# Layer-1 mixer: substitution of the 16x16 blocks per head group, spreads placed behind a convolution, second q-v-part last

## The chip, the cores and the metric

The kernel runs on one core of a Trainium2 chip. The metric is the device time of one execution in microseconds (us). Five instruction streams matter: TensorE (PE in the rows; its weight loads are PEld), VectorE (DVE), ScalarE (ACT), GpSimd (POOL) and SyncE (SP, which issues the weight loads). Each engine runs its own stream in order; a stream goes on when the semaphores that it waits for have come.

## The reference, cut to what matters

The reference is a trunk of two layers, each mixer, cross-attention and gated MLP with layer norms, on 256 tokens of width 1024. The change lies in the mixer of layer 1, a gated DeltaNet of 8 heads in chunks of 64 tokens:

```python
qkv = jax.nn.silu(causal_dwconv(jnp.concatenate([q, k, v], axis=-1), conv_w))   # width 4, per channel
m = jnp.where(strict, jnp.einsum('bhntk,bhnsk->bhnts', kb, kh) * decay, 0.0)
tinv = lax.linalg.triangular_solve(eye + m, eye, left_side=True, lower=True, unit_diagonal=True)
u = jnp.einsum('bhnts,bhnsv->bhntv', tinv, vh * beta[..., None])
w = jnp.einsum('bhnts,bhnsk->bhntk', tinv, kb * jnp.exp(gc)[..., None])
# over the chunks: v_new = u - w S;  out = qg S + qk v_new;  S = S * g_last + kg^T v_new
```

`q`, `k`, `v` and `z` come from one product of the tokens with `w_in`. For each head and chunk a unit lower triangular 64x64 matrix is inverted (`tinv`), which needs only `k` and the decays; `q` and `v` come in after it.

## The kernel before, in words

Eight heads are two groups of four (`grp`), 256 tokens are two tiles of 128 (`tt`); a unit of the chain below is one group and one tile, thus four heads by two chunks of 64.

TensorE's program in this mixer is written out by hand. `weave` runs a **chain** (the recurrence of `mixer_c`) and a **fill** (projections that nobody in the chain needs at once). Each yield of the chain says how many fill steps go in before its next part, and the table `NW` (L35) gives the weights; one step of a projection is six matmuls of 256 columns (`ps_t`, L159 to L161) or three of 512 (`ps_n`, L165 to L167). The fill is, in order, the projections q0, v0, q1, v1 (name and group), then z1. What the other engines do is put in their streams by a scheduler, roughly in the order in which the program names it. A projection piece of 24 matmuls costs VectorE and ScalarE this: ScalarE casts a weight block to `wh` (L152), VectorE takes the rest `wl` (L154), and when the piece's PSUM bank is full ScalarE starts the convolution `cv` (L927), VectorE adds three shifted terms (L930, called a convolution's three parts below) and ScalarE applies silu (L935). Such a bank is free again only after the third part, and there are four of them.

The chain, in the order of L1240 to L1262: `gdn_pre_k` of both groups makes the transposed matrix `LT` on VectorE (L1046), stores it to a scratch tensor in DRAM (`scr_in`, L1050, a queue of GpSimd) and transposes it back to `L`. `base_solve` (L1080 to L1099) loads the 128 diagonal 16x16 blocks, one on each partition (`base`, L1085), inverts them by substitution in 28 small instructions on GpSimd (L1087 to L1093), stores them (`scr_out`, L1094) and loads them back as `zc` with four DMAs, one per unit (L1099). `gdn_pre_q` makes what `q` and `v` give. `gdn_inv` first spreads `zc` into the block diagonal of `Z` (L1108, two instructions per unit on VectorE) and then doubles the block size in three levels: `pA` from `Z`, a masked copy `A` on VectorE, `pX`, a copy `X` on ScalarE, `pZ`, and `Z` anew on VectorE; at the end `pw`. `gdn_rec` is the recurrence over the chunks. All of VectorE's work for chain and fill stands in one stream.

The order is: pre_k of group 0, pre_k of group 1, one solve for both groups, wait for v0 in the fill, pre_q of group 0, wait for q1 in the fill, the inversion of group 0, wait for v1, pre_q of group 1, then the inversion of group 1 side by side with the recurrence of group 0, the rest of the fill, and the recurrence of group 1.

Of the kernel before, what the change touches and what calls it, by code (L numbers as in the profile page):

```python
# [10 lines left out]
F32 = mybir.dt.float32  # L11
# [3 lines left out]
ALU = mybir.AluOpType  # L15
AX = mybir.AxisListType

P = 128
D = 1024
KT = D // P  # L20
T = 256
# [8 lines left out]
BASE = 16  # L30
# [1 line left out]
LAG = 4  # L32
NEARLY = 6
AHEAD = 2
NW = [3, 2.6, 1, 1.5, 0.8, 1, 1, 1, 0.5, 8, 4, 1, 6, 2, 0, 5.2, 0.8, 3]  # L35
NEG = -1e30

def _constants():
# [51 lines left out]
def hybrid_trunk(ctx: ExitStack, tc: tile.TileContext, a: dict, const: dict, out: bass.AP, dbg=None):  # L90
    nc = tc.nc
# [7 lines left out]
    lnp = ctx.enter_context(tc.tile_pool(name="lnp", bufs=2))  # L99
# [26 lines left out]
    def C(name):  # L126
        group, c0, n = _COLS[name]
        return csb[group][:, c0:c0 + n]
# [40 lines left out]
    def run(gen):  # L169
        for _ in gen:  # L170
            pass
# [101 lines left out]
    def steps(n, *gens):  # L273

        gens = list(gens)
        while gens:
            due = 0
            for gen in list(gens):
                m = next(gen, gens)
                if m is gens:  # L280
                    gens.remove(gen)
                else:
                    due += n if m is None else m
            yield due
# [113 lines left out]
    def new_h():  # L398
        return [hp.tile([P, D], F32, tag="h", name="h") for _ in range(2)]
# [106 lines left out]
    def mixer_ab(h, hT, ap_, fill, res):  # L506
# [54 lines left out]
        with pool("gla") as sm:  # L561
# [124 lines left out]
            def intra(u):  # L686
# [4 lines left out]
                for l in range(NLEV + 1):  # L691
# [8 lines left out]
                    if l in (2, 4):  # L700
                        yield NW[14]
                pk = mm("pk")[:, :P]
# [36 lines left out]
            def gla():  # L739
# [7 lines left out]
                for i, u in enumerate(units):  # L747
                    yield from intra(u)
                    yield NW[15]
                    if i % 2:  # L750
# [28 lines left out]
            yield 0  # L779
            yield from steps(NW[1], gla())  # L780

# [87 lines left out]
    def mixer_c(h, hT, sm, smq, fill, res):  # L869
# [4 lines left out]
        cw = conv_w[0]  # L874
# [46 lines left out]
            table.append(nc.scalar.activation(egs.rearrange("p a b -> p (a b)"), pg[:, :32], AF.Exp))  # L921

        gate = [x.rearrange("p (t d) -> p t d", t=2) for x in new_h()]

        def conv_silu(dst, m, ps, late):
            y = smq.tile([P, T], F32, tag="cv", name="cv", bufs=4)
            nc.scalar.mul(y, ps, cw[:, 3, m:m + 1])  # L927
            for j in range(3):
                d = 3 - j
                nc.vector.scalar_tensor_tensor(y[:, d:], ps[:, :T - d], cw[:, j, m:m + 1], y[:, d:],  # L930
                                               op0=ALU.mult, op1=ALU.add)

            def finish():
                with tc.issue_after(table[0].ins):
                    table[1:] = [nc.scalar.activation(dst, y, AF.Silu)]  # L935
            late.append(finish) if late is not None else finish()
# [22 lines left out]
            return smq.tile(B4, F32, tag="t2", name=name, bufs=5)  # L959

        scr = ctx.enter_context(tc.tile_pool(name="scr", bufs=1, space=bass.MemoryType.DRAM))
        scr_in = scr.tile([16, P * (P + 1)], F32, name="scr_in")
        scr_out = scr.tile([P, BASE * BASE], F32, name="scr_out")

        os_ = [[{}, {}], [{}, {}]]

# [27 lines left out]
        tts = nc.vector.tensor_tensor  # L994
# [12 lines left out]
        def gdn_pre_k(grp, tt, o):  # L1007

            tsl = slice(tt * P, tt * P + P)
            cs = slice(tt * 8 + grp * 4, tt * 8 + grp * 4 + 4)  # L1010
            k = qkvT["k", grp][:, :, tsl]
            sc = o["sc"] = sm.tile([P, 6, 4], F32, tag="sc", name="sc", bufs=4)

            pg = bank("pg")
            mm4(pg, lambda g: gg[:, tt, grp * 4 + g:grp * 4 + g + 1].broadcast_to([P, P]), lambda g: tri)
            pk = bank("pk")
            tr4(pk, k)
            dT = o["att"] = keep("dT", grp, tt)
            for g in range(4):
                i = tt * 8 + grp * 4 + g  # L1020
                nc.vector.scalar_tensor_tensor(dT[:, g], pg[:, g], ngc[:, i:i + 1], dmask, op0=ALU.add, op1=ALU.min)
            with tc.issue_after(table[1].ins):
                nc.scalar.activation(dT, dT, AF.Exp)
                if tt:
                    qg = o["qg"] = keep("kq", grp, tt)
                    nc.scalar.activation(qg, pg, AF.Exp)
            sum_sq(sc[:, 0], pk)
            if tt:
                kgx = o["kgx"] = sm.tile(B4, F32, tag="kgx", name="kgx")
                tts(kgx, pk, col(egs[:, 0, cs]), op=ALU.mult)  # L1030
            else:
                kg = o["kg"] = keep("kq", grp, tt)
                tts(kg, pk, col(egs[:, 1, cs]), op=ALU.mult)
            yield


            nc.vector.tensor_scalar(sc[:, 0], sc[:, 0], RMS_EPS, None, op0=ALU.add)
            nc.gpsimd.tensor_tensor(sc[:, 2], sc[:, 0], phalf, op=ALU.pow)
            nc.vector.reciprocal(sc[:, 3], sc[:, 0])
            nc.vector.tensor_tensor(sc[:, 3], sc[:, 3], beta[:, tt, grp * 4:grp * 4 + 4], op=ALU.mult)  # L1040
            o["b"], o["eq"] = sc[:, 3], sc[:, 4]
            pK = bank("pK")
            mm4(pK, lambda g: k[:, g], lambda g: k[:, g])
            LT = t2("LT")
            for g in range(4):
                nc.vector.scalar_tensor_tensor(LT[:, g], pK[:, g], sc[:, 3, g:g + 1], dT[:, g],  # L1046
                                               op0=ALU.mult, op1=ALU.mult)
            yield

            nc.gpsimd.dma_start(scr_in[grp * 8 + tt * 4:grp * 8 + tt * 4 + 4, :P * P].rearrange("g (s t) -> s g t", t=P), LT)  # L1050
            pL = bank("pL")
            tr4(pL, LT)
            L = o["L"] = smq.tile(B4, F32, tag="L", name="L", bufs=4)
            nc.scalar.copy(L, pL)
            yield
# [21 lines left out]
            tts(dT, pQ, dT, op=ALU.mult)  # L1077
            yield

        def base_solve():  # L1080

            src = scr_in.rearrange("a b -> (a b)").rearrange("(p x) -> p x", x=BASE * (P + 1))
            src = src[:, :BASE * P].rearrange("p (i t) -> p i t", t=P)[:, :, :BASE]
            m, z = lnp.tile([P, 512], F32, tag="tok", name="base").rearrange("p (a i j) -> a p i j", a=2, j=BASE)
            nc.gpsimd.dma_start(m, src)  # L1085
            eng = nc.gpsimd
            eng.tensor_scalar(z, m, -1.0, None, op0=ALU.mult)  # L1087
            for i in range(1, BASE - 1):
                sh = [P, i, BASE - 1 - i]
                t = sm.tile([P, 64], F32, tag="bt", name="bt")[:, :sh[1] * sh[2]].rearrange("p (i j) -> p i j", i=i)  # L1090
                eng.tensor_tensor(t, z[:, :i, i:i + 1].broadcast_to(sh), m[:, i:i + 1, i + 1:].broadcast_to(sh), op=ALU.mult)
                eng.tensor_tensor(z[:, :i, i + 1:], z[:, :i, i + 1:], t, op=ALU.subtract)
            eng.memset(z.rearrange("p i j -> p (i j)")[:, ::BASE + 1], 1.0)  # L1093
            nc.gpsimd.dma_start(scr_out, z.rearrange("p i j -> p (i j)"))  # L1094
            back = scr_out.rearrange("(u g b) (i j) -> u (b i) g j", u=4, g=4, j=BASE)
            zc = sm.tile([P, 4, 4, BASE], F32, name="zc", bufs=1)
            for u in range(4):
                os_[u // 2][u % 2]["zc"] = zc[:, u]
                nc.gpsimd.dma_start(zc[:, u], back[u])  # L1099

        def gdn_inv(o):

            zc, L = o["zc"], o["L"]

            Z = o["Z"] = t2("Z")
            for u in range(2):
                sh = [P, 4, BASE, 4]
                tts(Z[:, :, 64 * u:64 * u + 64].rearrange("p g (r b) -> p g r b", b=4),  # L1108
                    zc.unsqueeze(3).broadcast_to(sh),
                    C("blocks")[:, 4 * u:4 * u + 4].unsqueeze(1).unsqueeze(1).broadcast_to(sh), op=ALU.mult)  # L1110
            for lev in range(4, NLEV + 1):

                last = lev == NLEV
# [30 lines left out]
                else:  # L1144
                    tts(Zv[:, :, :, 1], packed(Z[:, :, 64:]), packed(pZ), op=ALU.subtract)
                    Z = o["Z"] = Z2
# [82 lines left out]
        def until(nm, grp):  # L1229

            while (nm, grp) not in made:
                yield 1
            yield LAG

        def units(n, gen, grp, *args):
            return steps(n, *(gen(grp, tt, os_[grp][tt]) for tt in range(2)))

        def inv(grp):
            return [gdn_inv(os_[grp][tt]) for tt in range(2)]

        yield 0
        fill.gens += [fills(), proj_z(1)]
        yield from units(NW[3], gdn_pre_k, 0)
        yield from units(NW[5], gdn_pre_k, 1)
        base_solve()
        yield from until("v", 0)
        yield from units(NW[7], gdn_pre_q, 0)
        yield from until("q", 1)
        yield from steps(NW[4], *inv(0))
        yield from until("v", 1)  # L1250
        yield from units(NW[8], gdn_pre_q, 1)
        outs = []
        yield from steps(NW[16], *inv(1), gdn_rec(0, os_[0], outs))
        fill.rest()
        new = new_t("oT")
        oT.hi, oT.lo = new.hi, new.lo
# [2 lines left out]
        outs = []  # L1259
# [243 lines left out]
```

## Time and profile before

| | us |
|---|---|
| three runs | 935.9, 934.82, 934.26; median 934.82 |
| the profiled execution: its own time | 933.78 |
| its span in the trace | 931.9 |
| TensorE busy in it | 898.1 (96 %) |
| VectorE busy | 680.2 |
| ScalarE busy | 517.7 |
| GpSimd busy | 54.6 |

A time in a row counts from the span's start. A row of instructions in order of time gives its start, its length, engine, line, operation, tiles and the number merged into it; in brackets stands the idle time ahead of it and who ended that. "PEclk" is TensorE's granted clock as a share of full speed: 1.00 is 2.4 GHz, 0.50 is 1.2 GHz. A row on a stretch gives its bounds, its length, the busy time of PE, PEld, DVE, ACT and POOL (with the number of instructions), PEclk, the busy share of the DMA engines and what they moved in GB/s. Where TensorE is the bound, two things cost time: its idle time, and half of the time that it executes at 0.50.

### The profile page before, as it was taken

The page shows a single profiled execution, that of the slowest core. Times are in us where ns is not written, and L with a number is a line of the kernel's source. Part 1 is how long each engine was busy: PE and PEld are TensorE (multiplying, and loading weights), DVE is VectorE, ACT ScalarE, POOL GpSimd, SP SyncE. Part 2 cuts the span into 40 slices and gives each one's busy share as a digit, 9 for nine tenths or more (in the row PEclk, how much of TensorE's full clock was granted, in tenths as well). Part 3 has the DMA queues.
Part 4 walks back from the last instruction along what each step waited for, and adds up shares of the span by engine and source line. Part 5 has one row for each costly group of instructions (what it writes and reads, how often), then busy time and mean ns, then how long its engine had stood idle before and what let it go on. Part 6 is the DMA issues. An engine that isn't in the chain of part 4 may idle for free. (4 is left out here: it accounts for less than half of the span.)

```text
span 931.9 us, 15317 instructions
## 1 busy us (share of the span) xinstructions
PE 898.1 (96%) x6044; PEld 802.1 (86%) x6044; DVE 680.2 (73%) x1131; ACT 517.7 (56%) x907; POOL 54.6 (6%) x89
## 2 busy tenths in 40 slices
PE   6999999999999999999999996999999999999996
PEld 5877798889988999998889896888788789999885
DVE  6498586776458999984586985354796889999554
ACT  5753466445443867664356974463455376666440
POOL 1000001000000000000010152000200100000000
PEclk9999999999999999999999997898999999999999
DMA  8843345455673555665546453121543546655541
GB/s 256 299 137 119 108 136 184 178 181 168 195 240 120 181 181 190 206 205 204 193 145 202 140 165 102 46 91 46 180 147 126 180 139 223 216 193 185 195 164 46
DMA packets 102256, 154.10 MB, mean 165 GB/s; under 512 B 5385, under 2 KB 73833, under 8 KB 102185
## 3 DMA queue, kind: packets, MB, share of 16 engines
q1 hardware_dynamic: 99576, 145.08, 47.3%
q0 software_dynamic: 2608, 8.04, 2.8%
q8 instruction: 48, 0.79, 0.3%
q14 instruction: 24, 0.19, 0.1%
HBM read 150.88 MB, written 2.23 MB: 164 GB/s over the span
## 5 line engine op out<-in xcount | busy, mean ns | idle before, releaser
L154 DVE TENSOR_TENSOR wl<-raw,wh 128x1024 fp32r<-128x1024 f32 x268 | 325.7, 1224 | 116.9 <-ACT wh L152 114.4
L152 ACT CAST wh<-raw 128x1024 fp32r<-128x1024 f32 x268 | 278.8, 1052 | 219.5 <-PE ps_f L160 50.1
L161 PE MATMUL ps_f<-hT,wl 128*128 128x256 f32 x576 | 159.3, 277 | 0.0
L159 PE MATMUL ps_f<-hT,wh 128*128 128x256 f32 x576 | 159.3, 277 | 0.0
L160 PE MATMUL ps_f<-hT,wh 128*128 128x256 f32 x576 | 159.3, 277 | 0.0
L161 PEld LDWEIGHTS ps_f<-hT,wl 128*128 128x128 f32 x576 | 108.2, 188 | 0.0
L159 PEld LDWEIGHTS ps_f<-hT,wh 128*128 128x128 f32 x576 | 108.2, 188 | 0.0
L160 PEld LDWEIGHTS ps_f<-hT,wh 128*128 128x128 f32 x576 | 108.2, 188 | 0.0
L159 PE MATMUL ps_t<-hT,wh 128*128 128x256 f32 x352 | 101.2, 288 | 2.5 <-DVE cv L930 2.5
L160 PE MATMUL ps_t<-hT,wh 128*128 128x256 f32 x352 | 98.6, 280 | 0.0
L161 PE MATMUL ps_t<-hT,wl 128*128 128x256 f32 x352 | 98.5, 280 | 0.0
L159 PEld LDWEIGHTS ps_t<-hT,wh 128*128 128x128 f32 x352 | 67.2, 191 | 3.2 <-issue 2.7
L165 PE MATMUL ps_o<-wh,aT 128*128 128x512 f32 x176 | 69.2, 393 | 0.0
L166 PE MATMUL ps_o<-wl,aT 128*128 128x512 f32 x176 | 68.9, 392 | 0.0
L167 PE MATMUL ps_o<-wh,aT 128*128 128x512 f32 x176 | 68.7, 390 | 0.0
L160 PEld LDWEIGHTS ps_t<-hT,wh 128*128 128x128 f32 x352 | 67.2, 191 | 0.1
L161 PEld LDWEIGHTS ps_t<-hT,wl 128*128 128x128 f32 x352 | 67.0, 190 | 0.0
L303 PE MATMUL ps<-wh,hT 128*128 128x512 f32 x192 | 54.7, 403 | 0.0
L303 PEld LDWEIGHTS ps<-wh,hT 128*128 128x128 f32 x192 | 36.2, 192 | 8.4 <-DVE hT L382 0.5
L1364 ACT ACTIVATE fy<-ps_f,fcw 128x256 f32<-128x256 f32 x72 | 40.2, 559 | 0.0
L165 PEld LDWEIGHTS ps_o<-wh,aT 128*128 128x128 f32 x176 | 33.1, 188 | 7.6 <-issue 0.5
L136 POOL TENSOR_TENSOR lnmv<-lnmv,mhalf 128x1 f32<-128x1 f32 x12 | 11.4, 948 | 479.4 <-DVE lnmv L409 479.4
(366 smaller groups left out, 1811.1 us busy)
## 6 DMA issues: line engine op xcount, KB each, us to landing
raw<-in_ffn_w_in SPq DMA_DIRECT2D x44, 1024.0 KB, 5.4
raw<-in_w_in SPq DMA_DIRECT2D x26, 1024.0 KB, 5.6
raw<-in_ffn_w_out SPq DMA_DIRECT2D x22, 1024.0 KB, 5.0
raw<-in_xa_wkv SPq DMA_DIRECT2D x16, 1024.0 KB, 5.1
raw<-in_w_mix_out SPq DMA_DIRECT2D x8, 1024.0 KB, 5.0
raw<-in_xa_wq SPq DMA_DIRECT2D x8, 1024.0 KB, 7.3
raw<-in_xa_wo SPq DMA_DIRECT2D x8, 1024.0 KB, 5.3
lngb<-in_ln_g POOLq DMA_DIRECT2D x6, 512.0 KB, 4.4
```

The costliest lines, as they stand in the source:

```text
L136: nc.gpsimd.tensor_tensor(dst, src, mhalf[:, :n], op=ALU.pow)
L152: nc.scalar.copy(hi, src)
L154: nc.vector.tensor_tensor(lo, src, hi.bitcast(F32), op=ALU.subtract)
L159: nc.tensor.matmul(ps, lh, rh, start=first, stop=False)
L160: nc.tensor.matmul(ps, lh, rl, start=False, stop=False)
L161: nc.tensor.matmul(ps, ll, rh, start=False, stop=last)
L165: nc.tensor.matmul(ps, lh, rh, start=first, stop=False)
L166: nc.tensor.matmul(ps, lh, rl, start=False, stop=False)
L167: nc.tensor.matmul(ps, ll, rh, start=False, stop=last)
L303: nc.tensor.matmul(ps, x, ww[:, k], start=k0 + k == 0 and ww is wh and not xl, stop=k0 + k == KT - 1 and ww is wl)
L1364: nc.scalar.activation(yt, ps, AF.Identity, scale=cw[:, 2, mc:mc + 1], bias=cw[:, 3, mc:mc + 1])
```

## The change: what it does

The solve is made per group: two scratch tensors each way, 64 blocks on 64 partitions, the two loads back split off as `base_back`. Group 0's solve is run right behind its own pre_k; group 1's follows behind group 0's load back. Group 1's `LT` stores go out from ScalarE's queue and no longer from GpSimd's. The spread of `Z` is kept behind the last convolution part that the fill has recorded when the program comes to it (`last_conv`). The inversion of group 0 no longer waits for q1; the inversion of group 1 and the recurrence of group 0 come ahead of the wait for v1 and of pre_q of group 1, which is now last. Three weights in `NW` rise.

```diff
-NW = [3, 2.6, 1, 1.5, 0.8, 1, 1, 1, 0.5, 8, 4, 1, 6, 2, 0, 5.2, 0.8, 3]
+NW = [3, 2.6, 1, 1.5, 1.1, 1, 1, 1, 1, 8, 4, 1, 6, 2, 0, 5.2, 1, 3]
...
-                nc.vector.scalar_tensor_tensor(y[:, d:], ps[:, :T - d], cw[:, j, m:m + 1], y[:, d:],
-                                               op0=ALU.mult, op1=ALU.add)
+                last_conv[:] = [nc.vector.scalar_tensor_tensor(y[:, d:], ps[:, :T - d], cw[:, j, m:m + 1], y[:, d:],
+                                                               op0=ALU.mult, op1=ALU.add)]
...
-        scr_in = scr.tile([16, P * (P + 1)], F32, name="scr_in")
-        scr_out = scr.tile([P, BASE * BASE], F32, name="scr_out")
+        scr_in = [scr.tile([8, P * (P + 1)], F32, name=f"scr_in{i}") for i in range(2)]
+        scr_out = [scr.tile([64, BASE * BASE], F32, name=f"scr_out{i}") for i in range(2)]
...
-            nc.gpsimd.dma_start(scr_in[grp * 8 + tt * 4:grp * 8 + tt * 4 + 4, :P * P].rearrange("g (s t) -> s g t", t=P), LT)
+            (nc.scalar if grp else nc.gpsimd).dma_start(
+                scr_in[grp][tt * 4:tt * 4 + 4, :P * P].rearrange("g (s t) -> s g t", t=P), LT)
...
-        def base_solve():
+        def base_solve(grp):
...
-            nc.gpsimd.dma_start(m, src)
+            yield nc.gpsimd.dma_start(m, src)
...
-            nc.gpsimd.dma_start(scr_out, z.rearrange("p i j -> p (i j)"))
...
+            eng.dma_start(scr_out[grp], z.rearrange("p i j -> p (i j)"))
+
+        def base_back(grp):
+            back = scr_out[grp].rearrange("(u g b) (i j) -> u (b i) g j", u=2, g=4, j=BASE)
+            zc = sm.tile([P, 2, 4, BASE], F32, tag="zc", name="zc")
+            for u in range(2):
+                os_[grp][u]["zc"] = zc[:, u]
+                done = nc.gpsimd.dma_start(zc[:, u], back[u])
+            return done
...
-            for u in range(2):
+            with tc.issue_after(last_conv[0].ins):
+                for u in range(2):
...
         yield from units(NW[3], gdn_pre_k, 0)
+        first, second = base_solve(0), base_solve(1)
+        run(first)
         yield from units(NW[5], gdn_pre_k, 1)
-        base_solve()
+        with tc.issue_after(next(second).ins):
+            back = base_back(0)
+        with tc.issue_after(back.ins):
+            run(second)
+        base_back(1)
         yield from until("v", 0)
         yield from units(NW[7], gdn_pre_q, 0)
-        yield from until("q", 1)
         yield from steps(NW[4], *inv(0))
+        outs = []
+        yield from steps(NW[16], *inv(1), gdn_rec(0, os_[0], outs))
         yield from until("v", 1)
         yield from units(NW[8], gdn_pre_q, 1)
-        outs = []
-        yield from steps(NW[16], *inv(1), gdn_rec(0, os_[0], outs))
         fill.rest()
```

**VectorE at the first spread.** Before, behind one piece of the fill; each `L930` row is one part of a convolution, `c_m_4955` holds the masks:

```order
L930 SCALAR_TENSOR_TENSOR cv<-ps_t,gcw,cv 128x255
L1108 TENSOR_TENSOR Z<-zc,c_m_4955 128x4x64 x2
L1068 TENSOR_SCALAR sc<-sc 128x4
L1077 TENSOR_TENSOR dT<-pQ,dT 128x512 x2
L154 TENSOR_TENSOR wl<-raw,wh 128x1024
L930 SCALAR_TENSOR_TENSOR cv<-ps_t,gcw,cv 128x253
L930 SCALAR_TENSOR_TENSOR cv<-ps_t,gcw,cv 128x254
L930 SCALAR_TENSOR_TENSOR cv<-ps_t,gcw,cv 128x255
```

The same place of the stream now:

```order
L931 SCALAR_TENSOR_TENSOR cv<-ps_t,gcw,cv 128x255
L1070 TENSOR_SCALAR sc<-sc 128x4
L1079 TENSOR_TENSOR dT<-pQ,dT 128x512 x2
L154 TENSOR_TENSOR wl<-raw,wh 128x1024
L931 SCALAR_TENSOR_TENSOR cv<-ps_t,gcw,cv 128x253
L931 SCALAR_TENSOR_TENSOR cv<-ps_t,gcw,cv 128x254
L931 SCALAR_TENSOR_TENSOR cv<-ps_t,gcw,cv 128x255
L1114 TENSOR_TENSOR Z<-zc,c_m_4955 128x4x64 x2
L1132 TENSOR_TENSOR A<-pA,c_m_4955 64x256
L1114 TENSOR_TENSOR Z<-zc,c_m_4955 128x4x64 x2
L1132 TENSOR_TENSOR A<-pA,c_m_4955 64x256
```

The first unit's spread has moved behind `dT`, one `wl` and one more convolution; the second unit's stands behind the first unit's `A`, where before four pieces of the fill came between the two.

**VectorE at the end of group 0's inversion, now.** The last `Z` of group 0 (64x4x64, one per unit) and the first spread of group 1:

```order
L1149 TENSOR_TENSOR Z<-Z,pZ 64x4x64
L154 TENSOR_TENSOR wl<-raw,wh 128x1024
L931 SCALAR_TENSOR_TENSOR cv<-ps_t,gcw,cv 128x253
L1149 TENSOR_TENSOR Z<-Z,pZ 64x4x64
L931 SCALAR_TENSOR_TENSOR cv<-ps_t,gcw,cv 128x254
L1075 TENSOR_TENSOR kq<-kq,cq 128x512
L931 SCALAR_TENSOR_TENSOR cv<-ps_t,gcw,cv 128x255
L1114 TENSOR_TENSOR Z<-zc,c_m_4955 128x4x64 x2
L1132 TENSOR_TENSOR A<-pA,c_m_4955 64x256
```

Before, both last `Z` of a group stood among a `wl` and a convolution too, but no spread of the other group followed; pre_q of group 1 lay between.

**TensorE from pre_q of group 0 on.** Before, the chain's rows, with the fill's left out:

```order
L992 MATMUL pQ<-cq,ck 128x128 x8
...
L992 MATMUL pA<-Z,Lc 64x64 x4
L1129 MATMUL pX<-c_all,Z 64x128 x4
L992 MATMUL pA<-Z,Lc 64x64 x4
L1129 MATMUL pX<-c_all,Z 64x128 x4
...
L992 MATMUL pZ<-A,X 128x64 x8
```

Now, at the end of group 0's inversion:

```order
L993 MATMUL pZ<-A,X 64x64 x8
...
L993 MATMUL pw<-Z,kgx 128x128 x4
L993 MATMUL pA<-Z,Lc 64x64 x4
L1135 MATMUL pX<-c_all,Z 64x128 x4
L993 MATMUL pA<-Z,Lc 64x64 x4
L1135 MATMUL pX<-c_all,Z 64x128 x4
L993 MATMUL pvn<-vx,Z 128x128 x8
```

Before, 84 matmuls of the fill stood between `pQ` and the first `pA`; now 12 stand there. Within group 0's inversion 12, 12, 12, 12, 18 and 12 fill matmuls stand between the parts, the last 12 ahead of `pw`, and group 1's `pA` follows `pw` without any. TensorE's stream is the same again from `pz` of group 0 on, with the same number of instructions.

**GpSimd.** Before:

```order
L1038 TENSOR_TENSOR sc<-sc,phalf 128x4 x2
L1050 DMA scr_in<-LT 128x4x128 x2
L1085 DMA base<-scr_in 128x16x16
L1087 TENSOR_SCALAR base<-base 128x256
...
L1094 DMA scr_out<-base 128x256
L1099 DMA zc<-scr_out 128x4x16 x4
```

Now:

```order
L1051 DMA scr_in_4971<-LT 128x4x128 x2
L1087 DMA base<-scr_in_4971 64x16x16
L1089 TENSOR_SCALAR base<-base 64x256
...
L1039 TENSOR_TENSOR sc<-sc,phalf 128x4 x2
...
L1096 DMA scr_out_4973<-base 64x256
L1087 DMA base<-scr_in_4972 64x16x16
L1103 DMA zc<-scr_out_4973 128x4x16 x2
L1089 TENSOR_SCALAR base<-base 64x256
...
L1096 DMA scr_out_4974<-base 64x256
L1103 DMA zc<-scr_out_4974 128x4x16 x2
```

One chain of load, 28 instructions, store and load has become two behind each other, each with the same 28 instructions on half the partitions; group 1's two `sc` powers stand inside the first. SyncE's stream is the same.

## Rows read from the trace of the kernel before

**Rows 1.** Page: busy time, share of the span and instructions of TensorE and others.
```profile
PE 898.1 (96%) x6044; PEld 802.1 (86%) x6044; DVE 680.2 (73%) x1131; ACT 517.7 (56%) x907; POOL 54.6 (6%) x89
```
**Rows 2.** TensorE's waits, 480 to 705 us: total, times, longest in us.
```profile
PE pA L992 <- DVE Z L1108: 5.3, 1, 5.3
PE ps_t L159 <- DVE cv L930: 2.5, 1, 2.5
PE pw L992 <- DVE Z L1143: 2.1, 2, 1.1
PE pZ L992 <- DVE A L1124: 1.1, 1, 1.1
```
**Rows 3.** Stretches: length, busy PE, PEld, DVE, ACT, POOL, PEclk, DMA, GB/s.
```profile
560.03:643.13 83.10, 71.33 (x543) 63.12 (x543) 42.55 (x82) 38.91 (x101) 6.99 (x13) 0.88 0.22 70
572.29:589.36 17.07, 11.73 (x59) 10.43 (x58) 9.08 (x19) 6.79 (x15) 0.00 (x0) 0.50 0.31 111
640.55:647.38 6.83, 6.12 (x28) 6.12 (x29) 2.75 (x5) 1.97 (x3) 0.00 (x0) 0.50 0.45 154
```
**Rows 4.** VectorE in order of time, around the first spread.
```profile
549.29 1.35 DVE L154 TENSOR_TENSOR wl<-raw,wh 128x1024 fp32r<-128x1024 f32 x1
...
566.65 0.76 DVE L1108 TENSOR_TENSOR Z<-zc,c_m 128x256 f32<-128x256 f32 x2 [8.44 <-DMA zc<-scr_out]
...
567.40 1.28 DVE L1077 TENSOR_TENSOR dT<-pQ,dT 128x512 f32<-128x512 f32 x2
568.60 1.22 DVE L154 TENSOR_TENSOR wl<-raw,wh 128x1024 fp32r<-128x1024 f32 x1
...
572.29 1.51 DVE L930 SCALAR_TENSOR_TENSOR cv<-ps_t,gcw,cv 128x253 f32<-128x253 f32 x3
...
579.24 0.41 DVE L1108 TENSOR_TENSOR Z<-zc,c_m 128x256 f32<-128x256 f32 x1
579.58 0.68 DVE L1073 TENSOR_TENSOR kq<-kq,cq 128x512 f32<-128x512 f32 x1
```
**Rows 5.** GpSimd in order of time: stores, power, solve, load back.
```profile
526.42 0.76 POOL L1050 DMA_DIRECT2D scr_in<-LT  x1 [0.22 <-issue]
535.12 2.01 POOL L1038 TENSOR_TENSOR sc<-sc,phalf 128x4 f32<-128x4 f32 x2 [7.95 <-DVE sc L1037]
...
549.15 0.86 POOL L1087 TENSOR_SCALAR base<-base 128x256 f32<-128x256 f32 x1 [6.21 <-DMA base<-scr_in]
...
562.01 0.64 POOL L1094 DMA_DIRECT2D scr_out<-base  x1 [0.30 <-POOL base L1092]
564.38 2.99 POOL L1099 DMA_DIRECT2D zc<-scr_out  x4 [1.73 <-DMA scr_out<-base]
```
**Rows 6.** DMA issues, 505 to 660 us: count, KB each, median us to landing.
```profile
scr_in<-LT POOLq DMA_DIRECT2D x4, 256.0 KB, 3.4
base<-scr_in POOLq DMA_DIRECT2D x1, 128.0 KB, 7.3
scr_out<-base POOLq DMA_DIRECT2D x1, 128.0 KB, 2.1
zc<-scr_out POOLq DMA_DIRECT2D x4, 32.0 KB, 2.2
```
**Rows 7.** TensorE in order of time: the fill, then two later waits.
```profile
559.78 0.37 PE L159 MATMUL ps_t<-hT,wh 128*128 128x256 f32 x1
...
568.61 0.28 PE L161 MATMUL ps_t<-hT,wl 128*128 128x256 f32 x1
...
639.55 0.65 PE L992 MATMUL pZ<-A,X 64*64 64x64 f32 x8 [1.11 <-DVE A L1124]
...
641.26 2.08 PE L992 MATMUL pw<-Z,kgx 128*128 128x128 f32 x8 [1.05 <-DVE Z L1143]
```
**Rows 8.** ScalarE in order of time: two casts of weight blocks.
```profile
540.04 1.06 ACT L152 CAST wh<-raw 128x1024 fp32r<-128x1024 f32 x1 [1.36 <-PE ps_t L160]
...
560.65 1.05 ACT L152 CAST wh<-raw 128x1024 fp32r<-128x1024 f32 x1 [0.25 <-PE ps_t L160]
```

More of the change, by code (lines that the diff above doesn't have):

```diff
@@ L923, in mixer_c @@
         gate = [x.rearrange("p (t d) -> p t d", t=2) for x in new_h()]
+        last_conv = []
         def conv_silu(dst, m, ps, late):
@@ L1078, in gdn_pre_q @@
             yield
-        def base_solve():
-            src = scr_in.rearrange("a b -> (a b)").rearrange("(p x) -> p x", x=BASE * (P + 1))
+        def base_solve(grp):
+            src = scr_in[grp].rearrange("a b -> (a b)").rearrange("(p x) -> p x", x=BASE * (P + 1))
             src = src[:, :BASE * P].rearrange("p (i t) -> p i t", t=P)[:, :, :BASE]
-            m, z = lnp.tile([P, 512], F32, tag="tok", name="base").rearrange("p (a i j) -> a p i j", a=2, j=BASE)
-            nc.gpsimd.dma_start(m, src)
+            m, z = lnp.tile([P, 512], F32, tag="tok", name="base")[:64].rearrange("p (a i j) -> a p i j", a=2, j=BASE)
+            yield nc.gpsimd.dma_start(m, src)
             eng = nc.gpsimd
@@ L1088, in base_solve @@
             for i in range(1, BASE - 1):
-                sh = [P, i, BASE - 1 - i]
-                t = sm.tile([P, 64], F32, tag="bt", name="bt")[:, :sh[1] * sh[2]].rearrange("p (i j) -> p i j", i=i)
+                sh = [64, i, BASE - 1 - i]
+                t = sm.tile([64, 64], F32, tag="bt", name="bt")[:, :sh[1] * sh[2]].rearrange("p (i j) -> p i j", i=i)
                 eng.tensor_tensor(t, z[:, :i, i:i + 1].broadcast_to(sh), m[:, i:i + 1, i + 1:].broadcast_to(sh), op=ALU.mult)
@@ L1093, in base_solve @@
             eng.memset(z.rearrange("p i j -> p (i j)")[:, ::BASE + 1], 1.0)
-            nc.gpsimd.dma_start(scr_out, z.rearrange("p i j -> p (i j)"))
[L1095 to L1099, printed above, removed]
+            eng.dma_start(scr_out[grp], z.rearrange("p i j -> p (i j)"))
[6 more added lines that the diff above has]
+            return done
         def gdn_inv(o):
@@ L1105, in gdn_inv @@
             Z = o["Z"] = t2("Z")
-            for u in range(2):
[L1107 to L1110, printed above, removed]
+            with tc.issue_after(last_conv[0].ins):
+                for u in range(2):
+                    sh = [P, 4, BASE, 4]
+                    tts(Z[:, :, 64 * u:64 * u + 64].rearrange("p g (r b) -> p g r b", b=4),
+                        zc.unsqueeze(3).broadcast_to(sh),
+                        C("blocks")[:, 4 * u:4 * u + 4].unsqueeze(1).unsqueeze(1).broadcast_to(sh), op=ALU.mult)
             for lev in range(4, NLEV + 1):
```

## The prediction

> **What bounds the kernel now.** I read the page first: TensorE is busy for 96 % of the span [rows 1], so time can only be won where it idles or runs at the low clock. Then its waits over the mixer [rows 2], where the reader is to see that the long ones are all on VectorE: 5.3 us for a spread of `Z`, 2.5 us for a convolution, and four of about 1 us (`pw` twice, `pZ`, and one of 0.7 on ScalarE that isn't shown). Then the stretches [rows 3]. From 560.03 us (12 of the fill's matmuls after `pQ` have hardly begun) to 643.13 us (the end of `pw` of group 1) TensorE executes 71.33 of 83.10 us: 11.8 us idle. Two stretches have a granted clock of 0.50, thus 1.2 GHz: 572.29 to 589.36, where it executes 11.73 us, which costs half of that, 5.9 us, and 640.55 to 647.38 with 6.12 us, which costs 3.1 us. All that the change can remove is 11.8 + 5.9 + 3.1 = 20.8 us, of which it must not give back as much.
>
> Why VectorE is late is in its order of time [rows 4]: it waits 8.44 us, to 566.65, for the DMA of `zc`, with `dT`, `wl` and convolutions behind the spread. Four PSUM banks then fill up, and TensorE, which ran 78 of the fill's 84 matmuls at full speed from 559.78 to 568.61 (0.113 us from start to start [rows 7]), stops for 2.5 us. The second unit's spread, two instructions of 0.41 us around 579, comes behind the pieces that piled up: 5.3 us. The first stop is directly ahead of the fall of the clock at 572.3. The second fall, at 640.55, comes after 1.11 and 1.05 us idle within 3 us [rows 7].
>
> **The DMA chain, first.** Group 0's stores are issued by 527.2 and take 3.4 us [rows 5, 6], so they are down at about 530.5. The load of half the blocks isn't in the trace: I bound it by a store of LT's 3.4 us below and by the whole load's 7.3 us above, and take 7.3, its own kind: 537.8. The solve took 549.15 to 562.01, 12.9 us for 28 instructions; the same 28 on half the partitions are bounded by half of that and all of it, and I take all, since the small ones in the chain cost their start more than their width. Group 1's two powers, 2.01 us, stand inside. Store 2.1 us, issue 0.7, load back 2.2 us and another 0.75 us of issue (2.99 for four): `zc` of group 0 is there at 557 to 559, and by the lower bounds at about 547. The first spread can't start before 564 (below). The margin is 5 us or more, so the wait of 8.44 us on the DMA goes. Group 1's solve starts when its load has landed, follows on GpSimd behind the first, and gives `zc` by 572 to 579; its spread is wanted at 587 to 593. The two powers are late by 12 us but are only read in pre_q. Each spread's wait now costs nothing.
>
> In the Trainium skill, the page "DMA: Bandwidth & Descriptors", section "Rules for kernel authors", says that two transfers to disjoint halves of the partitions serialize, so that splitting one isn't worth it. No row here shows two such halves. By it the split wins nothing in the load, which is what I took; the sum stays as it is.
>
> The DMA issues of group 1's stores on ScalarE cost it 0.76 us each [rows 5], or about nothing at the lower bound. ScalarE is idle for 1.36 us ahead of its cast at 540.04 [rows 8], which hides one and half of the other; I take nothing, and 1 us at worst, which would be time of the fill.
>
> GpSimd's work lies beside more of VectorE's now: a `wl` beside the solve takes 1.35 us, one after it 1.22 [rows 4]. With two solves, some 5 of them are longer by 0.13: 0.6 us of VectorE, and as much off the path before 558, since VectorE isn't the bound there. For this and the stores I put 0.2 us in the sum.
>
> **What is late next: VectorE itself.** The inversion now starts 72 matmuls earlier, that is with the fill's pieces still coming in, and the spread is put behind a convolution.
>
> First spread. TensorE comes to `pA` 12 matmuls after 559.78, at 561.2. VectorE is by then done with `dT` (1.28 us). The cast that began at 560.65 ends at 561.70 [rows 8]; then come `wl` 1.22, three parts of a convolution 1.51 and the spread 0.76 [rows 4]: 565.2. TensorE waits 3.9 us, where it waited 2.5 at this place of the fill. (f) = 3.9.
>
> Clock. A stop of 2.5 us brought it down, so I expect 3.9 to. How long it stays low isn't settled by the rows; the two stretches bound it: 6.83 us, or 17.07 less the 5.3 idle within, thus 11.7 executing. It loses 3.4 to 5.9; I take the middle, (g) = 4.6.
>
> Second unit's spread. It stands directly behind `A`, with nothing of the fill between: 0.76 us, of which the first unit's `pX` hides most at the low clock. (h) = 0.2, at most 0.7.
>
> End of group 0. From the last fill matmul ahead of `pZ` the piece's cast takes 1.05 us, and VectorE must do `Z` 0.41, `wl` 1.22, three parts 1.51, `Z` 0.41, `kq` 0.68 and the spread 0.76, which end to start (each overlaps the next by some 0.07) is 4.5. Together 5.5 us. TensorE has `pZ` 0.65, 12 matmuls at 0.113 with their start, 1.4, and `pw`, half of the 2.08 of the row at the low clock [rows 7], so 3.0. It waits 2.5 us in two pieces, ahead of `pw` and ahead of group 1's `pA`, and 0.75 more for the second unit's spread, since at the full clock nothing hides it. (i) = 3.3, where `pw` cost 1.05 there before.
>
> Clock again. (i) is two or three idle pieces close together, as the 2.2 us ahead of 640.55 were. It likely falls, for 3.4 us lost at 6.83 us, or not at all; I take what the second stretch cost, (j) = 3.1.
>
> Last level of group 1. With `z1` as fill the convolutions are over and VectorE is lighter; I leave 0.75 of the 1.11 + 1.05 us. (k) = 0.75. pre_q of group 1, now between `z1` matmuls, was hidden before by the fill and is so now.
>
> Sum: 3.9 + 4.6 + 0.2 + 3.3 + 3.1 + 0.75 = 15.9 us in place of 20.8. With the 0.2 for GpSimd's and ScalarE's part the gain is 4.7: 933.78 − 4.7 = 929.1 for an execution such as the profiled one. The median of the runs lies 1.04 us above it, so 930.1.
>
> **The rivals.**
>
> A: the clock falls once and briefly. The second stop is in pieces, and each is shorter than the 2.5 that brought it down at first; against that stands 640.55, where pieces of 1.1 did. Without (j), and with (g) at 3.4: 15.9 − 3.1 − 1.2 = 11.6, a gain of 9.2: 925.6.
>
> B: the gain is eaten. VectorE's pieces come at 2.7 us per 24 matmuls (`wl` and three parts, 2.73 us), just as fast as TensorE makes them, 24 × 0.113 = 2.7 us, so each `A` and `Z` in between is pure delay for one of them; idle stays at 11.8 as before, and low stretches at 5.9 and 3.1 or so. Against it: chain parts of 2 to 4 us on TensorE stand between the pieces, in which VectorE catches up. About 934.8, no change.
>
> C, slower: VectorE never catches up within group 0, and so TensorE pauses again and again and the clock stays low while it executes. The stretch of 17.07 us then is one of execution throughout, at a cost of 8.5 us, and a second such follows behind (i): 3.9 + 0.2 + 3.3 + 0.75 + 2 × 8.5 = 25.2, that is 4.4 over before: 939.2. It decides from the point where the two low stretches together cost more than 12.6 us, 25 us of execution at 0.50. For it speaks that 78 matmuls of the fill now lie inside group 0's inversion; against it, that before the clock came back in the midst of such work, at 589.36.
>
> D: the change doesn't do what it says, as `zc` of group 1 is late behind the first solve and blocks VectorE as before. It would have to land after 593, 14 us later than by the upper bounds. About 934.
>
> **How the numbers follow.** The forecast 0.50, A 0.20, B 0.14, C 0.12, D 0.04. A measurement of this kernel tells 0.2 %, 1.9 us, from no change. The forecast, with the bounds of (g), (h) and (j), runs from 927.5 to 932.5, with most of it below 932.9; so faster is 0.47 + 0.20 + 0.03 = 0.70; same is B and D with a little of the forecast, 0.17; slower is C and the edge of B, 0.13. The range 924 to 936 holds the forecast, A and most of B and leaves C out.
>
> **What would show it.** Right: no wait of VectorE on the DMA of `zc`; TensorE's wait for the first spread of 3 to 5 us near 565; a stretch at 0.50 of 7 to 12 us behind it; waits at `pw` and group 1's `pA` of 2 to 3 us in all near 590; idle in the mixer of 8 to 9 us instead of 11.8. Wrong: the spread still ended by a DMA; a clock of 1.00 right through (then A and more); low stretches of over 25 us (C); or a wait on ScalarE's DMA issue near 540.

## The result and the profile after

The changed kernel takes 922.92 us (median of 4 runs, 921.79 to 924.13) against 934.54 of the kernel before beside it: ratio 0.9875, 95 % interval 0.9856 to 0.9893. Forecast were 930.1 us and a range of 924 to 936. The direction was right, the gain is 11.6 us instead of 4.4, and the time lies below the range. The profiled execution took 921.79 us, its span is 920.0.

TensorE's waits after, 480 to 705 us, against [rows 2] (total, times, longest):

```profile
PE pA L993 <- DVE Z L1114: 5.9, 4, 3.8
...
PE pw L993 <- DVE Z L1149: 0.3, 1, 0.3
```

Of the waits in the inversions and the recurrence, the four for the spread of `Z` and 0.3 us at `pw` are what is left; that for a convolution, that for `A` and two of about 1 us at `pw` are gone. In TensorE's order of time they stand here:

```profile
565.55 0.65 PE L993 MATMUL pA<-Z,Lc 128*64 128x64 f32 x8 [3.80 <-DVE Z L1114]
...
567.57 1.08 PE L993 MATMUL pA<-Z,Lc 128*64 128x64 f32 x8 [0.50 <-DVE Z L1114]
...
587.54 1.14 PE L993 MATMUL pZ<-A,X 64*64 64x64 f32 x16
590.60 1.16 PE L993 MATMUL pw<-Z,kgx 128*128 128x128 f32 x8 [0.31 <-DVE Z L1149]
592.65 0.68 PE L993 MATMUL pA<-Z,Lc 128*64 128x64 f32 x8 [0.89 <-DVE Z L1114]
...
594.60 0.65 PE L993 MATMUL pA<-Z,Lc 128*64 128x64 f32 x8 [0.71 <-DVE Z L1114]
```

The stretches after, against [rows 3]: from `pQ` to `pz` of group 0, then the low stretch, then the end of group 0's inversion:

```profile
558.43:634.39 75.96, 69.74 (x561) 62.53 (x560) 40.34 (x81) 39.91 (x111) 14.29 (x37) 0.96 0.25 82
...
566.32:573.15 6.83, 6.33 (x33) 5.42 (x32) 1.51 (x4) 2.31 (x5) 5.34 (x20) 0.50 0.28 109
...
590.60:603.00 12.40, 10.79 (x95) 10.04 (x96) 7.21 (x16) 5.45 (x11) 0.00 (x0) 1.00 0.05 8
```

The same piece of before:

```profile
558.08:643.13 85.05, 73.28 (x561) 65.07 (x560) 42.68 (x83) 40.86 (x112) 8.52 (x18) 0.88 0.22 72
```

Both have 561 matmuls. The piece is 9.1 us shorter: idle time fell from 11.8 to 6.2 us, and the rest is the clock. In this piece there is one stretch at 0.50 (1.2 GHz) left, with 6.33 us of execution, a loss of 3.2 us; the second one of before, which ended behind this piece at 647.38, is gone, and gives 2.1 us more. That is 11.2 of the 12.0 us between the two profiled executions; 0.8 us lies elsewhere and isn't explained.

VectorE no longer waits for the blocks; its spread follows the convolution's last part at once, as the order had it:

```profile
564.24 0.48 DVE L931 SCALAR_TENSOR_TENSOR cv<-ps_t,gcw,cv 128x255 f32<-128x255 f32 x1
564.64 0.76 DVE L1114 TENSOR_TENSOR Z<-zc,c_m 128x256 f32<-128x256 f32 x2
```

But GpSimd's rows, against [rows 5], show that this was close: the load back went out 6.5 us behind the store, and its 2.3 us bring the blocks to 564.5.

```profile
537.82 0.86 POOL L1089 TENSOR_SCALAR base<-base 64x256 f32<-64x256 f32 x1 [5.67 <-DMA base<-scr_in]
...
555.71 0.65 POOL L1096 DMA_DIRECT2D scr_out<-base  x1 [0.30 <-POOL base L1094]
556.36 0.85 POOL L1087 DMA_DIRECT2D base<-scr_in  x1
562.16 1.53 POOL L1103 DMA_DIRECT2D zc<-scr_out  x2 [4.94 <-issue]
563.71 0.88 POOL L1089 TENSOR_SCALAR base<-base 64x256 f32<-64x256 f32 x1
...
574.71 0.61 POOL L1096 DMA_DIRECT2D scr_out<-base  x1 [0.29 <-POOL base L1094]
```

From its first instruction to the store group 0's solve took 17.9 us, 2.0 of them for the two powers; group 1's took 11.0. The difference lies in seven of group 0's instructions, of 0.6 to 1.25 us each: each begins while VectorE runs a `wl` (six times) or a `kq` (once) and ends within 0.2 us of it. For two of them VectorE's row and then GpSimd's, with the next instruction:

```profile
546.24 2.50 DVE L154 TENSOR_TENSOR wl<-raw,wh 128x1024 fp32r<-128x1024 f32 x2
...
546.50 1.16 POOL L1094 TENSOR_TENSOR base<-base,bt 64x54 f32<-64x54 f32 x1
547.74 1.15 POOL L1093 TENSOR_TENSOR bt<-base 64x50 f32<-64x50 f32 x1
548.97 0.28 POOL L1094 TENSOR_TENSOR base<-base,bt 64x50 f32<-64x50 f32 x1
```

### The profile page after: what moved, and what is told of

It is laid out like the page before. It is cut to its first block, busy times and chain, and to the rows that moved or that the text cites. A ratio compares the mean times of both kernels' runs of the same rounds, so it can differ in the third digit from the quotient of the medians.

```text
span 920.0 us, 15346 instructions
## 1 busy us (share of the span) xinstructions
PE 891.8 (97%) x6044; PEld 796.8 (87%) x6044; DVE 679.8 (74%) x1131; ACT 517.4 (56%) x907; POOL 64.9 (7%) x119
```

## The experiments

Each was timed beside the kernel before on one chip; ratios are to that, with the 95 % interval. One execution of each was traced. For the others the record has the time and the mean granted clock over the span; twice what that clock lacks to 1.00, times the span, is an estimate of the time at 0.50, good to about 1 us.

**Which part carries the gain.** e1 keeps the split solve and the stores on ScalarE's queue and takes the order, the weights and the spread's place from before; e2 does the opposite, with one solve for both groups.

```diff
 e1, from the changed kernel
-NW = [3, 2.6, 1, 1.5, 1.1, 1, 1, 1, 1, 8, 4, 1, 6, 2, 0, 5.2, 1, 3]
+NW = [3, 2.6, 1, 1.5, 0.8, 1, 1, 1, 0.5, 8, 4, 1, 6, 2, 0, 5.2, 0.8, 3]
-            with tc.issue_after(last_conv[0].ins):
+        yield from until("q", 1)
         yield from steps(NW[4], *inv(0))
+        yield from until("v", 1)
+        yield from units(NW[8], gdn_pre_q, 1)
         outs = []
         yield from steps(NW[16], *inv(1), gdn_rec(0, os_[0], outs))
-        yield from until("v", 1)
-        yield from units(NW[8], gdn_pre_q, 1)
```

> Only the split of the solve, its early start for group 0 and group 1's stores from ScalarE's queue; the order of the chain, the weights NW and the place of the spread are those of before. Theory 1 (the gain comes from both, the early blocks and the new order): the blocks of group 0 land near 564.4 and not 566.7, so VectorE still waits some 4 to 5 us at the spread's old place, TensorE's stop of 2.5 us at the fill shrinks to about 0, the 5.3 us at the second unit shrink to about 3, and the two 1 us stops with the low stretch at the end of group 1 stay: 926 to 931. Theory 2 (the order alone carries the gain): 932 to 935. Theory 3 (the early blocks alone carry it): 921 to 925, no low stretch near 570.

Measured: 931.39 us, ratio 0.9967 (0.9950 to 0.9985). That is 0.4 above theory 1's range. VectorE still waits 6.4 us for the blocks at the spread's old place; the stop at the fill is gone, but the second unit's is 6.4 us, longer than before where 3 was expected, and both low stretches stay, of 13.7 and 3.4 us (17.1 and 6.8 before):

```profile
PE pA L993 <- DVE Z L1113: 6.4, 1, 6.4
PE pw L993 <- DVE Z L1148: 2.1, 2, 1.1
PE pZ L993 <- DVE A L1129: 1.1, 1, 1.1
```

> Only the order of the chain, the weights and the spread kept behind the convolution; one solve for both groups on 128 partitions, where it was. Theory 1: the blocks land at 566.7, two us later than the convolution ends, so TensorE's first stop is 5.5 to 6 us and not 3.8, the low stretch behind it as in the changed kernel (6 us at 0.50), the later stops as there: 924 to 927. Theory 2: 922 to 924. Theory 3: 931 or more.

Measured: 927.3 us, ratio 0.9929 (0.9908 to 0.9949), 0.3 above theory 1's range. The first stop was 11.1 us, twice what I expected: VectorE waited 7.2 us for the blocks, which landed later than in the trace of before. In e8, the same kernel traced again, it waited 4.8 us for them, and the stop was 8.7 us. So the order alone gives some 6.6 us, the split alone 3, together 11 to 12; neither alone is enough, and theories 2 and 3, whose ranges both runs miss, fall.

**The spread's place.** e3 drops `issue_after(last_conv[0].ins)` in the changed kernel.

```diff
-            with tc.issue_after(last_conv[0].ins):
-                for u in range(2):
+            for u in range(2):
```

> The changed kernel without keeping the spread behind the convolution; the scheduler puts the first unit's spread ahead of dT, wl and the convolution. If keeping it there matters: VectorE waits from 560 to 564.5 for the DMA and does dT, wl and the convolution after it, the first pA starts at 565.3 all the same, and later A, second spread and fill are 2 to 3 us late: 924.5 to 927. If the blocks' landing alone sets the first stop: 922 to 924, like the changed kernel.

Measured: 925.12 us, ratio 0.9898 (0.9868 to 0.9929). In the trace VectorE waits 5.8 us for the blocks and TensorE stops for 3.4 and 3.0 us where it had 3.8 and 0.5, which is the pattern that was expected of a place that matters. The first `pA` starts at 567.3, and all of this trace before the mixer's inversions is 1.8 us later than the changed kernel's, so that is close to the expected 565.3. In time it isn't told apart from the changed kernel, whose interval overlaps, so what the place is worth isn't shown.

**The first stop.** e4 puts 30 fill matmuls ahead of the first `pA`.

```diff
         yield from units(NW[7], gdn_pre_q, 0)
+        pin[:] = last_conv
+        yield 5
         yield from steps(NW[4], *inv(0))
+        pin.clear()
...
-            with tc.issue_after(last_conv[0].ins):
+            with tc.issue_after((pin or last_conv)[0].ins):
```

> The changed kernel with 30 more matmuls of the fill (3.4 us) between pQ and the first pA, the spread still behind the same convolution as in the changed kernel. If the stop of 3.8 us and the 6 us at 0.50 behind it belong together: the first is 0 to 0.5 us, no low stretch near 570, a stop of 1 to 2 us at the second unit's spread, which now has a convolution ahead of it: 917 to 919. If the stop only moves to the second unit and the clock falls all the same: 922 to 925.

Measured: 919.29 us, ratio 0.9843 (0.9823 to 0.9862). The stop of 3.8 us became 0.49, the second unit's spread, behind a convolution now, cost 2.17 us, and the clock still fell, at 570, for 3.4 us. The first expectation missed the clock and by little the time; the stop moved in part.

e5 puts the spreads of both units together in a function `spread(o)`, group 0's ahead of `yield 5`, group 1's ahead of group 0's last level; e9 runs group 1's behind both `A` copies of that level.

```diff
 e5, from e4
+        with tc.issue_after(last_conv[0].ins):
+            for o in os_[0]:
+                spread(o)
         yield 5
...
                 last = lev == NLEV
+                if last and at:
+                    at()          # spread(o) for o in os_[1]
 e9, from e5
-                if last and at:
-                    at()
...
                 yield
+                if last and at:
+                    at()
                 pZ = mm("pZ")[cols, :256]...
```

> The kernel of the run before this (30 more fill matmuls ahead of the first pA), and both units' spreads of a group stand together: group 0's behind the same convolution, group 1's ahead of the last level of group 0's inversion. If the stops behind the spreads are what is left and what brings the clock down: no stop over 1 us from 560 to 640, no stretch at 0.50 near 570, 912.5 to 916. If VectorE's load itself is the limit, the waits move to A or to group 1's blocks, which land near 579.5: 917 to 920.

Measured: 921.68 us, ratio 0.9856 (0.9829 to 0.9882), above both expected ranges. The first stop is 0.55 us and the clock stays at 1.00 there, but VectorE waits 5.6 us for group 1's blocks, TensorE 2.42 us for a `Z` behind them, and then the clock falls:

```profile
560.00:583.00 23.00, 20.19 (x179) 18.65 (x177) 14.18 (x29) 13.29 (x30) 14.55 (x35) 1.00 0.36 111
584.00:590.00 6.00, 6.00 (x34) 5.39 (x32) 3.30 (x8) 3.52 (x7) 0.00 (x0) 0.50 0.01 3
```

> As the kernel with the spreads together, but group 1's spreads one part later, behind both copies of A of group 0's last level, some 5 us after its blocks have landed. If in the kernel with the spreads together only the wait for these blocks (a stop of 2.4 us and a stretch at 0.50 behind it) stood in the way: stops under 1 us each, the clock at 1.00 throughout the mixer, 913.5 to 916.5. If the clock falls on such small stops as well or VectorE is late in another place: 918 to 922.

Measured: 917.69 us, ratio 0.9823 (0.9799 to 0.9848), the fastest version, though not told apart from e4, and between the two expectations. Its profiled execution is its slowest, 923.11 us: group 0's blocks landed late there, VectorE waited 3.6 us for them, TensorE stopped for 2.1 and 1.7 us, and a stretch at 0.50 of 13.7 us followed. The other five, 915.58 to 919.09, weren't traced, but their mean clocks are 0.993 to 0.998 against 0.990: an estimate of 4 to 13 us at 0.50 each, where the traced one has 18. The fastest has 4 us, no more than the 4.4 us that the traced one has at the end of its span, where TensorE does nothing any more. So it had most likely no low stretch in the mixer.

**Weights and queue.** e6 gives the changed kernel the old weights, e7 issues all `LT` stores from GpSimd.

```diff
 e6
-NW = [3, 2.6, 1, 1.5, 1.1, 1, 1, 1, 1, 8, 4, 1, 6, 2, 0, 5.2, 1, 3]
+NW = [3, 2.6, 1, 1.5, 0.8, 1, 1, 1, 0.5, 8, 4, 1, 6, 2, 0, 5.2, 0.8, 3]
 e7
-            (nc.scalar if grp else nc.gpsimd).dma_start(
+            nc.gpsimd.dma_start(
```

> The changed kernel with the three weights of before: 6 fill matmuls and not 12 ahead of each pZ and of pw in group 0's inversion, and 12 for 18 around group 1's. If the second fall of the clock hangs on the stops at the end of group 0: 0.7 us more in each of some four places, stops of 2.5 to 3.5 us there in place of 1.9, a stretch at 0.50 near 590 in most runs: 927 to 930. If the weights hardly matter: 922 to 924.5.

Measured: 926.4 us, ratio 0.9916 (0.9889 to 0.9943). The stretch at 0.50 near 590 did not come: the stops there were 1.07 and 0.71 us. Its first stop was 5.1 us with a wait of 1.2 us for the blocks, which the weights don't touch, and a stretch at 0.50 of 17.1 us followed, so how much the weights are worth in time stays open. One thing the trace does show: at group 1's `pw` TensorE stops for 1.04 us again, where the changed kernel, with more fill there, had no wait.

> The changed kernel with group 1's LT stores issued from GpSimd's queue, where they stand behind the first solve's store. The load of group 1's blocks then waits for them, and group 0's load back, which is kept behind it, too. If the margin of group 0's blocks at the first spread is as small as it looks (they land at 564.4, the convolution ends at 564.7): the first spread waits for the DMA 3 to 6 us, TensorE's first stop is 7 to 10 us: 926 to 930. If there is room, as the prediction had it (5 us): 922 to 924.5.

Measured: 927.38 us, ratio 0.9926 (0.9906 to 0.9947). VectorE waits 5.4 us for the blocks, TensorE 9.4 us for the first spread. There was no room: a delay of the blocks is paid at once.

**The second fall of the clock.** e8 is e2's kernel traced once more, e11 the changed kernel, and e10 takes the 12 fill matmuls ahead of `pw` away from the changed kernel.

```diff
 e10
                     Z = o["Z"] = Z2
-                yield
+                yield 0 if last and any(o is x for x in os_[0]) else None
```

> The kernel of e2 once more for its trace: there the same three stops (0.34, 0.90, 0.71 us) near 599 as in the changed kernel's trace were followed by a stretch at 0.50, which they weren't there. If that second fall is left to chance at this size of stop, this trace may have none and then is 3 to 4 us shorter, near 925.5; if it is a matter of what lies before, it falls again and the time is 928 to 930.

Measured: 926.04 us. The three stops at the end of group 0 (0.35, 0.89, 0.71 us) are those of e2, and yet e2's clock fell behind them, for 3.4 us, and e8's didn't. First e2, then e8, from the last of the stops on:

```profile
601.50:605.00 3.50, 3.50 (x22) 3.27 (x22) 0.59 (x2) 1.15 (x3) 0.00 (x0) 0.55 0.00 0
```

```profile
598.70:605.00 6.30, 6.30 (x58) 6.11 (x59) 2.07 (x3) 2.82 (x6) 0.00 (x0) 1.00 0.00 0
```

> The changed kernel once more, beside the two others. If the second stretch at 0.50 at this size of stops comes in some executions and not in others: a spread of the times of 3 us or more, 921 to 925, and its trace may have the stretch near 595. If it never comes: times within 2 us of 922.5 and no such stretch.

Measured: 923.24 us, ratio 0.9885 (0.9854 to 0.9915), 920.12 to 929.64. The slowest execution has a mean clock of 0.986 where the traced one (922.9 us) has 0.995: an estimate of 26 us at 0.50 for 10, enough for the 6.7 us between them. The low clock thus differs from execution to execution of one kernel; whether the slowest had the second stretch isn't known. The trace has the same three stops and a clock of 1.00 behind them. It also has a wait of 1.5 us for the blocks at the second unit's spread and a stop of 2.15 us there, where the first trace had no wait and 0.50 us.

> The changed kernel without the 12 fill matmuls between group 0's last pZ and pw (they come later); VectorE's order is the same. The stops at the end of group 0 grow from 1.9 to the 3.3 us that the prediction had there. If that size brings the clock down, as the prediction said of it: a stretch at 0.50 behind 590, 1.4 for the stops and about 3 for the clock, 926 to 929. If the clock stays up even so, the step from stops to clock was wrong and not the size of the stops: 923.5 to 925.

Measured: 925.1 us, ratio 0.9895 (0.9872 to 0.9917), 1.9 above e11's median, below what was expected. The stops grew to 1.92, 0.89 and 0.28 us, and the clock fell, behind the first two of them:

```profile
591.11 1.16 PE L993 MATMUL pw<-Z,kgx 128*128 128x128 f32 x8 [1.92 <-DVE Z L1149]
593.16 1.11 PE L993 MATMUL pA<-Z,Lc 128*64 128x64 f32 x8 [0.89 <-DVE Z L1114]
595.55 1.08 PE L993 MATMUL pA<-Z,Lc 128*64 128x64 f32 x8 [0.28 <-DVE Z L1114]
```

```profile
593.15:596.56 3.41, 3.12 (x20) 2.39 (x21) 1.08 (x3) 1.41 (x4) 0.00 (x0) 0.50 0.00 0
```

It executed 3.12 us there, so the fall itself cost 1.6 us. The intervals of e10 and e11 overlap, and its trace has a stop of 2.9 us at the second unit's spread besides, behind a wait of 2.0 us for the blocks; what shows the fall is this one trace, and not the time.

**Where the margin of the blocks went.** e12 issues group 0's load back ahead of group 1's load; e13 is the same edit on e9.

```diff
-        with tc.issue_after(next(second).ins):
-            back = base_back(0)
+        back = base_back(0)
```

> The changed kernel with group 0's load back issued ahead of group 1's load on GpSimd's queue, and nothing else. The prediction gave the store 2.1 us; in the changed kernel's trace the load back is issued 6.5 us after the store's issue began (555.7 to 562.2). If group 1's load behind the store in the queue made it late: the load back goes out 2.3 us after the store, the blocks are there near 560.5, no wait of VectorE on them, and 921 to 923. If the weight loads that run at the same time made it late: the load back goes out at 561 to 562 as before, waits of 1 to 2 us on it in some executions, 922 to 925; group 1's blocks are later by some 3 us in both, and are not missed.

Measured: 921.48 us, ratio 0.9856 (0.9835 to 0.9876). The load back still goes out 6.7 us behind the store, with group 1's load now behind it in the queue. That load is not the cause. VectorE waits 2.5 us for the blocks at the second unit's spread, and TensorE stops there for 3.3 us behind a first stop of 4.0; the three stops at the end of group 0 are the same as before (0.34, 0.89, 0.71 us), and the clock stays at 1.00 behind them. The two stretches from store to load back, group 0's and group 1's:

```profile
554.65:561.39 6.74, 5.87 (x51) 5.54 (x49) 4.08 (x9) 6.47 (x29) 0.65 (x1) 1.00 0.53 168
580.58:582.85 2.27, 2.27 (x19) 2.20 (x20) 0.76 (x2) 0.00 (x0) 0.61 (x1) 1.00 0.13 29
```

The slow one has 168 GB/s of transfers beside it, the quick one 29; in the changed kernel it is 6.45 us beside 185 GB/s and 2.28 beside 29. The two traces of e2's kernel (e2 and e8) show the same once more, for a store of 128 KB: first e2's store and its load back up to the first spread, then e8's.

```profile
565.58:570.63 5.05, 0.00 (x0) 0.00 (x0) 0.13 (x1) 0.42 (x1) 0.64 (x1) 0.71 0.65 227
570.63:572.92 2.29, 0.00 (x0) 0.00 (x0) 0.00 (x0) 0.00 (x0) 2.29 (x4) 0.50 0.14 20
```

```profile
562.29:564.65 2.36, 0.00 (x0) 0.00 (x0) 2.29 (x4) 0.05 (x1) 0.64 (x1) 1.00 0.34 75
564.65:569.48 4.83, 0.00 (x0) 0.00 (x0) 0.01 (x2) 0.42 (x1) 3.00 (x4) 0.62 0.73 235
```

In one execution the store is slow, in the other the load back, each time the one with over 220 GB/s beside it. That VectorE's work beside it is the cause, the other rival, is out: in the quick store it is busy for 2.29 of 2.36 us and in the two slow ones for 0.13 and 0.01. So the weight loads beside it go with the delay; no run took them away.

> The same edit on the kernel with 30 more fill matmuls and group 1's spreads one part later. If it brings group 0's blocks early: no stop over 1 us up to 640, clock 1.00 in the mixer, 913.5 to 916.5 in nearly all executions; group 1's blocks land near 583 and its spreads at 586 don't wait. If the blocks stay late: 916 to 919, as without the edit, with stops of 2 us and a stretch at 0.50 in some executions.

Measured: 922.68 us, ratio 0.9856 (0.9824 to 0.9887), times from 914.86 to 924.87, above both expectations. In the trace the blocks stayed late: a wait of 3.5 us for them, a stop of 3.01 us at the second unit and a stretch at 0.50 from 571 to 584. That the mixer would be free of stops with early blocks is thus not tested by a trace.

## Why the prediction was wrong, point by point

- What bounds the kernel, and the DMA wait at the spread: right. The wait of 8.44 us is gone, and VectorE sets the next stop.
- The blocks of group 0, 5 us ahead of need: wrong. They came at 564.5, with no margin, some 6 us later than the prediction's 557 to 559. The load did land at 537.8, as said. Two steps behind it failed, about 3 us and 4 us. The solve with the powers was put at 14.9 us and took 17.9: the prediction priced what GpSimd's work does to VectorE's `wl` (0.13 us each) and left out the reverse, some 0.9 us for each GpSimd instruction that began beside a `wl`. And the store was put at 2.1 us from [rows 6], which beside the weight loads took some 6. All this cost nothing in the changed kernel's first trace and 1.5 us of waiting in the second.
- The load of half the blocks, bounded by 3.4 and 7.3 us and put at 7.3: it took 5.9 us (median of the two) in the changed kernel, beside other transfers. The Trainium skill's page "DMA: Bandwidth & Descriptors", section "Rules for kernel authors", sees no gain in two halves, since they serialize. Here the two halves were never in flight together (531 to 538 and 556 to 562 us), so no run tests that rule.
- (f), the first stop: 3.80 us for 3.9. Right in mechanism and size.
- (g), the clock behind it: it fell as expected, for 6.8 us, and lost 3.2 where 4.6 were taken and 3.4 was the lower bound; in e11 it was again 6.8 us and lost 2.3, since a stop lay within. The other bound, 11.7 us of execution, came out of a stretch with a stop of 5.3 us within; long stretches are real (e1: 11.7 us of execution behind one stop, 577.4 to 589.1), and what sets their length wasn't found.
- (h): 0.50 for 0.2, within its bound.
- (i), the end of group 0: 1.91 us for 3.3. The step that failed is the work that TensorE has in hand while VectorE does the piece. I put it at 3.0 us and counted `pZ` of one unit, 0.65; the cast starts at 587.53, at the same time as `pZ` of both units, 1.14 us, and with the 12 matmuls (1.7 for 1.4) and `pw` (1.16 for 1.0) TensorE has 3.9 us in hand. VectorE's part was 5.1 us and not 5.5, as the first `Z` was done beside the cast and not behind it. The second unit's 0.75 was right (0.71).
- (j), the second fall, "It likely falls", 3.1 us: it didn't come. This is the largest term of the miss, 3.1 of 6.5 us. The step that failed is the one from small stops close together to a fall of the clock, taken over from 640.55. The three stops of 1.9 us in all were followed by a stretch at 0.50 in one trace of six (e2; not in the changed kernel's two, e7, e8 and e12). With 3.1 us of stops in this place the clock did fall in the one trace that there is (e10). That the prediction's 3.3 us would have brought it down is thus likely and not shown, and what decides it stays open. Its price was too large as well: the falls in e2 and e10 cost 1.7 and 1.6 us.
- (k): 0 for 0.75. TensorE had no wait at all there. It isn't `z1` as fill alone that did it, as the prediction had it: e6 has `z1` there too, and with the old weights, thus less fill ahead of `pw`, it stops for 1.04 us.

Sum of what was left: 3.8 + 3.2 + 0.5 + 1.9 = 9.4 us, for 15.9. (g), (i), (j) and (k) were all put too high, by 1.4, 1.4, 3.1 and 0.75. Rival A (a chance of 0.20) was the case that came, and below its 925.6 because (i) and (k), which A held fast, were smaller too; the range, whose lower end lay only 1.6 us under A's time, had no room for that. The forecast's own bounds were too narrow by its own words: with (j) at nothing, which it allowed ("or not at all"), and (g) and (h) at their lower bounds, it comes to 925.6 and not to 927.5. Rivals B and C, VectorE never catching up, fall with the waits after: none for `A`, none at the fill. D falls with the row at 564.64 in the first trace; e11 has a little of it, for group 0 and not group 1.

## What to carry to other kernels

Count the work that the waiting engine still has in hand for all units that stand between the two, not for one. Price the low clock behind a stop as a term with a chance of its own that hangs on the stop, for it came behind small stops in some executions and not in others. A DMA whose time comes from a quiet row should be priced again for what runs beside it in its new place, and so should a chain on GpSimd for what VectorE does beside it. In a stream that is served in order, take the thing that waits out of the way of those that don't, and put other work of the bound engine where it has to wait.

## What was not expected of the hardware

A store of 64 KB and the wait for its landing took 2.3 us beside 29 GB/s and 6.5 to 6.7 us beside 168 to 185 GB/s. Instructions of the substitution on GpSimd that began beside a `wl` of VectorE lasted until that one was over, up to 1.25 us in place of 0.2 to 0.3; half the partitions did not make the substitution much shorter (11.0 us with no `wl` beside it, against 12.9 with three instructions so held up on all 128 partitions). The same kernel with the same three stops (0.3, 0.9, 0.7 us) had a stretch of low clock behind them in one execution and none in another; stretches at 0.50 lasted from 3.4 us (e4, e10's second) to 17.1 us (e6, with a second stop within), and no run showed what decides it.
